# The first norm of a two-layer mixer: shifts as matrix-vector products on TensorE, dot products on VectorE, part of the squares summed on TensorE

## Chip, cores and metric

The program runs on one core of a Trainium2 chip. The metric is the device time of one execution in microseconds (us). A core has a matrix engine (TensorE, PE in the rows, with its weight loads as PEld), a vector engine (VectorE, DVE), a scalar engine (ScalarE, ACT) and a general one (GpSimd, POOL); SyncE (SP) issues the loads. Each takes its instructions in the order in which they were put into its queue and waits for semaphores at the head of the queue.

## What is computed

The reference holds two transformer blocks in sequence; the second follows the first in the same program and is not touched. The change concerns the first norm of the first block's first layer (`S` = 512 tokens, `D` = 1024 channels, all in float32):

```python
def rmsnorm(x, g):
    y = x * lax.rsqrt(jnp.mean(x * x, axis=-1, keepdims=True) + EPS)
    return y * g

c_act = jax.nn.silu(c)
for l in range(DEPTH):
    mod = (c_act @ ada_w[l] + ada_b[l])[:, None, :]
    sh1, sc1, g1, sh2, sc2, g2 = jnp.split(mod, N_MOD, axis=-1)
    h = rmsnorm(x, norm1_g[l]) * (1.0 + sc1) + sh1
    x = x + g1 * token_mix(h, w_in[l], ...)
    ...
```

`token_mix` begins with `h @ w_in`, from which the queries, keys, values and gates of a retention are taken. So the stage needs 1024 shifts (`sh1`) and 1024 scales (`sc1`), each a dot product of 1024 elements with `c_act`, a root of a mean for each token, the normed `h`, and then the first projections.

## The kernel before

**Tiles.** The activations lie transposed: `x[k]`, k = 0 to 7, holds 128 channels on the partitions and 512 tokens along the row. `h[k]` is a pair of such tiles, a high part `hh` (float32 rounded to the matrix engine's fp32r type) and a low part `hl` (what the rounding left). Weights are split the same way: ScalarE makes the high part by a copy (`whi` at L123 for a tile of 128x1024; `yrh` at L140 for halves of 128x512 that are held over the stage), VectorE the low part by a subtraction (`wlo` L124, `yrl` L141). A product in `mm` is three products of 128x128 by 128x512: L151 (hi by hi), L152 (hi by the low part of h), L154 (the low part of the weight by hi).

**The stage `start0` (L923).** It is the head of the program. SyncE loads `x`, a row of `c` for all partitions (`crow`, silu applied), blocks of `ada_w` and the weights.

- Squares: ScalarE squares the eight `x[k]` (L930, L933), VectorE adds them up in seven additions (L934). `rstd_bcast` then sums the result over the partitions by four products with one moving column, one for every 128 tokens (L185), takes the root in seven small operations on VectorE (L164 to L175), and broadcasts it by four products of 128x128 (L193). The broadcast, `R`, stays in the accumulator memory.
- Scales and shifts: a block of `ada_w` comes transposed, 128 channels on the partitions and the 1024 elements of `c` along the row. `mod1` makes one dot product on VectorE (L265: multiply by `crow` and accumulate, 128x1024). Scales (block 8+k) all go this way, and shifts (block k) for k = 0 and 1. For k of 2 and above GpSimd multiplies the shift's block by `crow` (L964) and ScalarE sums the row (L966). Bias additions of 128x1 (L974) and the factor `gm` (L975) follow on VectorE.
- h: `t = x[k]*gm*R` on VectorE (L978), `hh = t + shift` on ScalarE (L979), `hl` on VectorE (L980).
- Products: with each h[k], `mm` for six output tiles: two of queries (weights by `first_w`, one low part on VectorE, one on GpSimd), two of keys and two of gates (weights by `held_w`, split in halves). That is 6 outputs x 8 k x 3 = 144 products of 128x512.

Behind the stage the value projections follow on TensorE; their first product is at L618.

**What sets the order.** The functions only record the work; a scheduler puts the recorded instructions into the queue of each engine, and pools of buffers bound how early a load may go: six slots hold blocks of `ada_w` (pool `stp`), four the raw weights (`raw`). In the queues, an instruction that waits holds up all that stand behind it.

The line that makes a shift for k of 2 and above before:

```python
                pool_e.tensor_tensor(ada[k], ada[k], crow, op=ALU.mult)
                junk = T(D, dt=BF16)
                act.activation(junk, ada[k], AF.Copy, accum_out=raw[:, k:k + 1])
```

Of the kernel before, what the change touches and what calls it, by code (L numbers as in the profile page):

```python
# [11 lines left out]
F32 = mybir.dt.float32  # L12
# [7 lines left out]
P = 128  # L20
# [36 lines left out]
def tile_two_blocks(ctx: ExitStack, tc: tile.TileContext, I, out):  # L57
# [16 lines left out]
    def nm(s):  # L74
        uid[0] += 1
        return f"{s}_{uid[0]}"
# [447 lines left out]

    crow = silu_row(I["c"], crp)
    def x_tile(dt=F32):
        return xp.tile([P, KD * S], dt, tag="x", name=nm("xb"))
# [8 lines left out]
    stp = sts.enter_context(tc.tile_pool(name="stp", bufs=6, side="right"))  # L536

    def ada_load(i):
        t = stp.tile([P, D], F32, tag="ada", name=nm("ada"))
        sp.dma_start(t, I["adaT"][0][i])  # L540
        return t

    ada = {i: ada_load(i) for i in (8, 0)}
# [379 lines left out]
    def start0(mp):  # L923
# [3 lines left out]
        acc = T(S, "t")  # L927
        for k in range(KD):
            if k == 0:
                act.activation(acc, x[k], AF.Square)  # L930
            else:
                sq = T()
                act.activation(sq, x[k], AF.Square)  # L933
                dve.scalar_tensor_tensor(acc, acc, EPS * D / P if k == 1 else 0.0, sq, op0=ALU.add, op1=ALU.add)  # L934
        R = rstd_bcast([(acc, 0)], S)
# [4 lines left out]
        def first_w(m):  # L940
            w = wload(win[m], D, eng=pool_e if m % 2 else dve)
            wks.append([wk(w, k) for k in range(KD)])
# [13 lines left out]
        ada[9], ada[1] = ada_load(9), ada_load(1)  # L956
        held_w(16)
        held_w(17)
        for k in range(KD):
            mod1(0, [8 + k], [ada[8 + k]])  # L960
            if k < 2:
                mod1(0, [k], [ada[k]])
            else:
                pool_e.tensor_tensor(ada[k], ada[k], crow, op=ALU.mult)  # L964
                junk = T(D, dt=BF16)
                act.activation(junk, ada[k], AF.Copy, accum_out=raw[:, k:k + 1])  # L966
            if 2 <= k + 2 < KD:
                ada[10 + k], ada[2 + k] = ada_load(10 + k), ada_load(2 + k)
# [3 lines left out]
            o = COFF["adab"]  # L972
            for i in (8 + k, k):
                dve.tensor_tensor(mod[:, i:i + 1], raw[:, i:i + 1], cols[:, o + i:o + i + 1], op=ALU.add)  # L974
            dve.scalar_tensor_tensor(gm[:, k:k + 1], mod[:, 8 + k:9 + k], 1.0, col("n1g", k),  # L975
# [601 lines left out]
def host_layout(i):  # L1577
# [4 lines left out]
    d["c"] = i["c"].reshape(1, D)  # L1582
    d["c2"] = i["c_2"].reshape(1, D)
# [57 lines left out]
```

## Time and profile before

| | |
|---|---|
| median of three runs | 2994.58 us (2992.69 to 2999.7) |
| profiled execution, its own time | 2997.35 us |
| its span, first to last instruction | 2995.5 us |
| granted clock of TensorE, mean of the span | 0.988 of full |
| TensorE busy | 2913.6 us, 97% |
| VectorE busy | 2128.8 us, 71% |
| ScalarE busy | 1160.0 us, 39% |
| GpSimd busy | 188.3 us, 6% |
| stage `start0` on TensorE | to 73.03 us, start of the first value product |

All rows are of one profiled execution, and their times are microseconds from the start of the span. Busy time counts the instructions that compute. PEclk is the clock that TensorE was granted, as a share of full speed. A float32 product of TensorE that is not of the fp32r type is recorded twice, and with two weight loads, so the four products of L185 stand in the timeline as x8. Operands of TensorE stand as moving data first, then what is loaded as weights; the shape at the end is the output's. Numbers of buffers are left out, and each `ada` is another block. The times of matrix products overlap with their successor's, so the time from start to start is what one of them takes from the next.

### The profile page before, as it was taken

To read this page: it belongs to the slowest core of one execution; us is meant where nothing else is said; L and a number is where in the kernel's file an instruction comes from. 1 tells how busy PE (TensorE), PEld (TensorE's weight loads), DVE (VectorE), ACT (ScalarE), POOL (GpSimd) and SP (SyncE) were. 2 spreads that over 40 slices of the span, in tenths; PEclk is the share of its full clock that TensorE was granted. 3 is DMA by queue.
4 is the path that set the end of the run, shared out by engine and by line. 5 is a ranking of instruction groups with operands and counts; after the bars stand their busy time and mean duration, and the time that the engine had idled before them with its cause. 6 is when DMAs were issued, how large, how long until landed. Compare 5 with 4: busy or idle time off the path is not lost.

```text
span 2995.5 us, 42050 instructions
## 1 busy us (share of the span) xinstructions
PE 2913.6 (97%) x16432; PEld 2562.8 (86%) x16432; DVE 2128.8 (71%) x3765; ACT 1160.0 (39%) x1997; POOL 188.3 (6%) x137
## 2 busy tenths in 40 slices
PE   6999999999999999999999999999999899899998
PEld 4888888988889888888888888999999777899997
DVE  7766455777767665556788878677777767686786
ACT  4333333433344332324433345323334446444442
POOL 2000001000000000002000010000001280200001
PEclk9999999999999999999999999999999899999999
DMA  6444254265553333344355532122224210313331
GB/s 249 126 128 130 96 155 145 89 195 187 187 161 101 116 98 121 120 140 142 114 176 182 168 115 76 64 64 71 71 70 149 70 63 15 99 43 105 107 112 59
DMA packets 119160, 350.41 MB, mean 117 GB/s; under 512 B 12496, under 2 KB 26448, under 8 KB 118960
## 3 DMA queue, kind: packets, MB, share of 16 engines
q1 hardware_dynamic: 117808, 346.67, 36.2%
q8 instruction: 129, 2.11, 0.3%
q10 hardware_dynamic: 1152, 1.05, 0.1%
q14 instruction: 71, 0.58, 0.1%
HBM read 343.48 MB, written 4.19 MB: 116 GB/s over the span
## 4 chain that ended last, share of the span: by engine, by line
PE 91%; DVE 6%; ACT 1%; issue 1%; DMA 1%; POOL 0%; DVEq 0%; SPq 0%; ACTq 0%; POOLq 0%
PE mm L151 28%; PE mm L154 27%; PE mm L152 27%; PE sm L185 1%; PE mm L1438 1%; PE mm L618 1%; PE mm L620 1%; PE mm L619 1%; PE sm L193 1%; DVE acc L219 1%; PE mm L1419 1%; DVE wlo L124 0%; DVE hl L236 0%; PE mm L1241 0%; PE mm L1242 0%
## 5 line engine op out<-in xcount | busy, mean ns | idle before, releaser
L123 ACT ACTIVATE whi<-raw 128x1024 fp32r<-128x1024 f32 (+3 forms) x471 | 453.9, 965 | 775.2 <-PE mm L152 520.3
L151 PE MATMUL mm<-hh,whi 128*128 128x512 f32 (+2 forms) x1956 | 723.7, 371 | 6.5 <-ACT hh L979 4.7
L154 PE MATMUL mm<-hh,wlo 128*128 128x512 f32 (+2 forms) x1956 | 722.9, 370 | 1.4 <-POOL wlo L124 1.4
L152 PE MATMUL mm<-hl,whi 128*128 128x512 f32 (+2 forms) x1956 | 721.7, 369 | 2.2 <-DVE hl L236 2.2
L124 DVE TENSOR_TENSOR wlo<-raw,whi 128x1024 fp32r<-128x1024 f32 (+3 forms) x450 | 497.6, 1111 | 260.8 <-ACT whi L123 256.3
L151 PEld LDWEIGHTS mm<-hh,whi 128*128 128x128 f32 x1956 | 369.6, 189 | 69.6 <-ACT hh L979 5.2
L152 PEld LDWEIGHTS mm<-hl,whi 128*128 128x128 f32 x1956 | 370.2, 189 | 62.3 <-DVE hl L236 3.0
L154 PEld LDWEIGHTS mm<-hh,wlo 128*128 128x128 f32 x1956 | 369.6, 189 | 60.5 <-POOL wlo L124 2.1
L151 PE MATMUL mm<-dh,whi 128*128 128x512 f32 (+1 forms) x760 | 274.8, 362 | 0.0
L152 PE MATMUL mm<-dh,whi 128*128 128x512 f32 (+1 forms) x760 | 268.5, 361 | 0.0
L154 PE MATMUL mm<-dh,wlo 128*128 128x512 f32 (+1 forms) x760 | 251.6, 362 | 0.0
L265 DVE SCALAR_TENSOR_TENSOR t<-ada,crow 128x1024 bf16<-128x1024 f32 x202 | 244.7, 1216 | 6.5 <-DMA ada<-adaT 5.9
L124 POOL TENSOR_TENSOR wlo<-raw,whi 128x1024 fp32r<-128x1024 f32 x21 | 51.7, 2484 | 2309.7 <-ACT whi L123 1764.9
L151 PEld LDWEIGHTS mm<-dh,whi 128*128 128x128 f32 x760 | 143.0, 188 | 29.4
L152 PEld LDWEIGHTS mm<-dh,whi 128*128 128x128 f32 x760 | 142.9, 188 | 23.3
L154 PEld LDWEIGHTS mm<-dh,wlo 128*128 128x128 f32 x760 | 133.1, 188 | 16.7
L847 DVE SCALAR_TENSOR_TENSOR t<-mm,cols,t 128x511 f32<-128x511 f32 (+1 forms) x96 | 70.6, 735 | 73.4 <-ACT t L846 73.0
L151 PE MATMUL mm<-tc,whi 128*128 128x256 f32 (+1 forms) x386 | 113.5, 294 | 0.0
L154 PE MATMUL mm<-tc,wlo 128*128 128x256 f32 (+1 forms) x386 | 112.5, 292 | 0.0
L152 PE MATMUL mm<-tc,whi 128*128 128x256 f32 (+1 forms) x368 | 106.6, 290 | 0.0
L1111 DVE TENSOR_TENSOR z<-z,mm 128x512 f32<-128x512 f32 (+1 forms) x112 | 67.2, 607 | 51.4 <-PE mm L154 51.0
L846 ACT ACTIVATE t<-mm,cols 128x512 f32<-128x512 f32 (+1 forms) x96 | 73.0, 760 | 74.4 <-PE mm L154 74.4
(477 smaller groups left out, 5877.8 us busy)
## 6 DMA issues: line engine op xcount, KB each, us to landing
ada<-adaT SPq DMA_DIRECT2D x96, 512.0 KB, 3.8
raw<-winT SPq DMA_DIRECT2D x96, 512.0 KB, 3.6
raw<-upT SPq DMA_DIRECT2D x88, 512.0 KB, 3.7
raw<-up2T SPq DMA_DIRECT2D x88, 512.0 KB, 3.5
ada<-wmodT SPq DMA_DIRECT2D x72, 512.0 KB, 4.4
raw<-down2T SPq DMA_DIRECT2D x30, 512.0 KB, 4.0
raw<-downT SPq DMA_DIRECT2D x32, 384.0 KB, 3.3
raw<-downT SPq DMA_DIRECT2D x32, 320.0 KB, 3.3
```

The costliest lines, as they stand in the source:

```text
L123: act.activation(hi[:p, :n], raw, AF.Copy)
L124: (eng or dve).tensor_tensor(lo[:p, :n], raw, f(hi[:p, :n]), op=ALU.subtract)
L151: pe.matmul(ps, lhsT=wh, rhs=r[k][0], start=first and k == 0, stop=False, skip_group_check=more)
L152: pe.matmul(ps, lhsT=wh, rhs=r[k][1], start=False, stop=False, skip_group_check=more)
L154: pe.matmul(ps, lhsT=wl, rhs=r[k][0], start=False, stop=last and k == n - 1, skip_group_check=more)
L185: pe.matmul(pm[:, t:t + 1], lhsT=sq[:, t * P:(t + 1) * P], rhs=meanc[:, mc:mc + 1], start=False, stop=i == len(parts) - 1 and t == nt - 1)
L193: pe.matmul(pr[:, t * P:(t + 1) * P], lhsT=y[:, t:t + 1].to_broadcast([P, P]), rhs=identL, start=True, stop=True)
L219: dve.tensor_tensor(acc, acc, sq, op=ALU.add)
L265: dve.scalar_tensor_tensor(junk, raw[:, :D], 1.0, vec, op0=ALU.mult, op1=ALU.mult, accum_out=dst[:, i:i + 1])
L846: act.activation(t, ps, AF.Identity, bias=col(bname, bi), scale=col(wname, taps[1] + wi))
L847: dve.scalar_tensor_tensor(t[:, 1:n], ps[:, 0:n - 1], col(wname, taps[0] + wi), t[:, 1:n], op0=ALU.mult, op1=ALU.add)
L1111: dve.tensor_tensor(zz, zz, ps, op=ALU.add)
```

## The change

Shifts: for all eight k, the block of `ada_w` is loaded in its own orientation (`adaN`, elements of `c` on the partitions) beside the transposed block for the scale, and the shift is eight matrix-vector products on TensorE, each with a 128x128 block as the loaded side and one column of `silu(c)` (`ccol`) as the moving side, all into one column of the accumulator `psh` (L964 in the kernel after). ScalarE adds the bias on its way out (L966). `ccol` is a new small load with its own sigmoid and multiplication.

Scales: the eight dot products on VectorE stay; the bias, plus one, is added once for all (`adab1`), so that `gm` reads the raw dot product. GpSimd does nothing in the stage: its multiplications for the shifts, ScalarE's sums and GpSimd's low part of the second weight go, the last to VectorE.

Squares: `sumsq` with `tail=3` has VectorE add the first five tiles (four additions) and leaves the last three to TensorE, which sums four tiles over the partitions in 16 products instead of one tile in four.

Buffers: the blocks come in pairs, two pairs ahead, from eight slots instead of six.

```diff
--- before.py
+++ after.py
@@ -522,7 +522,12 @@
         pend()
 
 
+    ccol = cst.tile([P, KD], F32, name="ccol")
+    csg = T(8, "se", bufs=4)
+    sp.dma_start(ccol, I["cT"])
     crow = silu_row(I["c"], crp)
+    act.activation(csg, ccol, AF.Sigmoid)
+    dve.tensor_tensor(ccol, ccol, csg, op=ALU.mult)
     def x_tile(dt=F32):
         return xp.tile([P, KD * S], dt, tag="x", name=nm("xb"))
 
@@ -533,14 +538,16 @@
     for k in range(KD):
         sp.dma_start(x[k], I["xT"][:, k * S:(k + 1) * S])
     sts = ExitStack()
-    stp = sts.enter_context(tc.tile_pool(name="stp", bufs=6, side="right"))
-
-    def ada_load(i):
-        t = stp.tile([P, D], F32, tag="ada", name=nm("ada"))
-        sp.dma_start(t, I["adaT"][0][i])
-        return t
-
-    ada = {i: ada_load(i) for i in (8, 0)}
+    stp = sts.enter_context(tc.tile_pool(name="stp", bufs=8, side="right"))
+
+    def ada_load(k):
+
+        ts = [stp.tile([P, D], F32, tag="ada", name=nm("ada")) for _ in (0, 1)]
+        sp.dma_start(ts[0], I["adaT"][0][8 + k])
+        sp.dma_start(ts[1], I["adaN"][k])
+        return ts
+
+    ada = [ada_load(0)]
     cols = cst.tile([P, NCOLS], F32, name="cols")
     sp.dma_start(cols, I["cols"])
     mods = []
@@ -924,21 +931,16 @@
 
 
         raw, mod, gm = mods[0]
-        acc = T(S, "t")
-        for k in range(KD):
-            if k == 0:
-                act.activation(acc, x[k], AF.Square)
-            else:
-                sq = T()
-                act.activation(sq, x[k], AF.Square)
-                dve.scalar_tensor_tensor(acc, acc, EPS * D / P if k == 1 else 0.0, sq, op0=ALU.add, op1=ALU.add)
-        R = rstd_bcast([(acc, 0)], S)
+        R = rstd_bcast(sumsq(x, S, tail=3), S)
+        psh = PS(KD, "sm")
+        adab1 = T(8, "sq1", bufs=4)
+        dve.tensor_scalar(adab1, cols[:, COFF["adab"] + 8:COFF["adab"] + 16], 1.0, None, op0=ALU.add)
         h = hq["h"] = hslots(S)
         win = I["winT"][0]
         wks, pss = [], []
 
         def first_w(m):
-            w = wload(win[m], D, eng=pool_e if m % 2 else dve)
+            w = wload(win[m], D)
             wks.append([wk(w, k) for k in range(KD)])
 
         def held_w(m):
@@ -953,26 +955,21 @@
 
         first_w(8)
         first_w(9)
-        ada[9], ada[1] = ada_load(9), ada_load(1)
+        ada.append(ada_load(1))
         held_w(16)
         held_w(17)
         for k in range(KD):
-            mod1(0, [8 + k], [ada[8 + k]])
-            if k < 2:
-                mod1(0, [k], [ada[k]])
-            else:
-                pool_e.tensor_tensor(ada[k], ada[k], crow, op=ALU.mult)
-                junk = T(D, dt=BF16)
-                act.activation(junk, ada[k], AF.Copy, accum_out=raw[:, k:k + 1])
-            if 2 <= k + 2 < KD:
-                ada[10 + k], ada[2 + k] = ada_load(10 + k), ada_load(2 + k)
+            mod1(0, [8 + k], [ada[k][0]])
+            for i in range(KD):
+                pe.matmul(psh[:, k:k + 1], lhsT=ada[k][1][:, i * P:(i + 1) * P], rhs=ccol[:, i:i + 1],
+                          start=i == 0, stop=i == KD - 1)
+            act.activation(mod[:, k:k + 1], psh[:, k:k + 1], AF.Identity, bias=col("adab", k))
+            if k + 2 < KD:
+                ada.append(ada_load(k + 2))
             if k == 1:
                 held_w(24)
                 held_w(25)
-            o = COFF["adab"]
-            for i in (8 + k, k):
-                dve.tensor_tensor(mod[:, i:i + 1], raw[:, i:i + 1], cols[:, o + i:o + i + 1], op=ALU.add)
-            dve.scalar_tensor_tensor(gm[:, k:k + 1], mod[:, 8 + k:9 + k], 1.0, col("n1g", k),
+            dve.scalar_tensor_tensor(gm[:, k:k + 1], raw[:, 8 + k:9 + k], adab1[:, k:k + 1], col("n1g", k),
                                      op0=ALU.add, op1=ALU.mult)
             tt = T()
             dve.scalar_tensor_tensor(tt, x[k], gm[:, k:k + 1], R, op0=ALU.mult, op1=ALU.mult)
@@ -1580,6 +1577,8 @@
     d["xT"] = i["x"][0].T.reshape(KD, P, S).transpose(1, 0, 2).reshape(P, KD * S)
     d["ctxT"] = i["ctx_2"][0].T.reshape(KD, P, CTX).transpose(1, 0, 2).reshape(P, KD * CTX)
     d["c"] = i["c"].reshape(1, D)
+    d["cT"] = i["c"].reshape(KD, P).T
+    d["adaN"] = i["ada_w"][0][:, 0:D].reshape(KD, P, KD, P).transpose(2, 1, 0, 3).reshape(KD, P, D)
     d["c2"] = i["c_2"].reshape(1, D)
     d["cc"] = i["c_ctx_2"].reshape(1, D)
     pack = {
```

The scheduler places the new instructions as follows. On TensorE, at the head of the program before (`zero`, `meanc` and `identL` are constants, `sm_154` the summed squares, `sm_171` the broadcast, `mm_243` and `mm_247` the two query outputs):

```order
L182 MATMUL sm_154<-zero 128x4
L185 MATMUL sm_154<-meanc,t_131 128x1 x4
L193 MATMUL sm_171<-identL,sy_160 128x128 x4
L182 LDWEIGHTS zero
L182 MATMUL sm_1053<-zero 128x4
L151 MATMUL mm_243<-hh_176,whi_194 128x512
L151 MATMUL mm_247<-hh_176,whi_200 128x512
L152 MATMUL mm_243<-hl_177,whi_194 128x512
```

and after (`acc_136` is the sum of five squares, `t_150` to `t_154` the last three; `ada_117` and `ada_222` are the blocks of the first and second shift):

```order
L185 MATMUL sm_156<-meanc,acc_136 128x1 x4
L185 MATMUL sm_156<-meanc,t_150 128x1 x4
L185 MATMUL sm_156<-meanc,t_152 128x1 x4
L185 MATMUL sm_156<-meanc,t_154 128x1 x4
L193 MATMUL sm_185<-identL,sy_174 128x128 x4
L964 MATMUL sm_190<-ccol,ada_117 128x1 x8
L151 MATMUL mm_265<-hh_193,whi_211 128x512
L152 MATMUL mm_265<-hl_194,whi_211 128x512
L154 MATMUL mm_265<-hh_193,wlo_212 128x512
L151 MATMUL mm_269<-hh_193,whi_217 128x512
L152 MATMUL mm_269<-hl_194,whi_217 128x512
L154 MATMUL mm_269<-hh_193,wlo_218 128x512
L964 MATMUL sm_190<-ccol,ada_222 128x1 x8
```

Three groups of four products have come ahead of the broadcast, and eight matrix-vector products stand ahead of the first product with h; the next eight stand behind the last product of k = 0.

On ScalarE, from the last square on, before:

```order
L933 ACTIVATE t_151<-xb_99 128x512
L123 ACTIVATE whi_194<-raw_192 128x1024
L979 ACTIVATE hh_176<-t_239,mod_118 128x512
L123 ACTIVATE whi_200<-raw_198 128x1024
L140 ACTIVATE yrh_210<-raw_208 128x512
L140 ACTIVATE yrh_214<-raw_208 128x512
L979 ACTIVATE hh_178<-t_290,mod_118 128x512
```

and after:

```order
L210 ACTIVATE t_154<-xb_104 128x512
L966 ACTIVATE mod_123<-sm_190,cols 128x1
L976 ACTIVATE hh_193<-t_261,mod_123 128x512
L123 ACTIVATE whi_211<-raw_209 128x1024
L123 ACTIVATE whi_217<-raw_215 128x1024
L966 ACTIVATE mod_123<-sm_190,cols 128x1
L976 ACTIVATE hh_195<-t_317,mod_123 128x512
```

The high part of the first weight (`whi`) stood ahead of the first h tile and now stands behind it and behind the shift's bias (L966).

On VectorE the first dot product stood ahead of the root and the second within it; now one dot product stands within the root, ahead of its last step, and none ahead of it.

On TensorE in the middle of the stage, from the last product of k = 3 to the first ones of k = 4, before:

```order
L152 MATMUL mm_307<-hl_183,yrh_279 128x512
L154 MATMUL mm_307<-hh_182,yrl_280 128x512
L151 MATMUL mm_243<-hh_184,whi_194 128x512
L152 MATMUL mm_243<-hl_185,whi_194 128x512
L154 MATMUL mm_243<-hh_184,wlo_195 128x512
```

and after (k = 4 is `hh_201`; `ada_347` and `ada_397` are the blocks of the shifts of k = 4 and 5):

```order
L154 MATMUL mm_334<-hh_199,yrl_309 128x512
L964 MATMUL sm_190<-ccol,ada_347 128x1 x8
L964 MATMUL sm_190<-ccol,ada_397 128x1 x8
L151 MATMUL mm_265<-hh_201,whi_211 128x512
L151 MATMUL mm_269<-hh_201,whi_217 128x512
```

Two groups of eight matrix-vector products stand back to back between the products of k = 3 and those of k = 4.

## Rows read from the trace of the kernel before

**Rows 1.** page part 1: busy us of each engine, share of span, instructions.

```profile
PE 2913.6 (97%) x16432; PEld 2562.8 (86%) x16432; DVE 2128.8 (71%) x3765; ACT 1160.0 (39%) x1997; POOL 188.3 (6%) x137
```

**Rows 2.** stretches: from:to, length, busy us (instructions) of PE, PEld, DVE, ACT, POOL, PEclk, DMA, GB/s.

```profile
20.00:30.00 10.00, 4.51 (x8) 2.29 (x8) 9.93 (x10) 2.60 (x4) 8.36 (x3) 1.00 1.03 402
40.00:50.00 10.00, 6.84 (x26) 5.26 (x27) 9.67 (x9) 4.99 (x10) 5.14 (x2) 0.94 0.43 156
```

**Rows 3.** TensorE's waits, 0 to 140 us: total us, times, longest us.

```profile
PE sm L185 <- DVE t L934: 11.6, 1, 11.6
PE mm L154 <- DVE yrl L141: 7.5, 2, 4.6
PE mm L151 <- ACT hh L979: 4.7, 2, 3.2
```

**Rows 4.** timeline of TensorE: start, us, line, operation, operands, xcount, [idle before <-releaser].

```profile
48.79 0.74 PE L154 MATMUL mm<-hh,yrl 128*128 128x512 f32 x1 [2.90 <-DVE yrl L141]
...
73.03 0.28 PE L618 MATMUL mm<-whi,hh 128*128 128x256 f32 x1
```

**Rows 5.** chain of waits, 45 to 60 us: start, us until the next, what.

```profile
49.53 0.43 PE mm L151
...
53.17 0.23 PE mm L152
...
59.93 0.23 PE mm L151
```

**Rows 6.** timelines of GpSimd (first row) and VectorE.

```profile
21.64 3.36 POOL L124 TENSOR_TENSOR wlo<-raw,whi 128x1024 fp32r<-128x1024 f32 x1 [20.34 <-ACT whi L123]
...
22.84 2.18 DVE L974 TENSOR_TENSOR mod<-modr,cols 128x1 f32<-128x1 f32 x1
...
30.60 1.28 DVE L141 TENSOR_TENSOR yrl<-raw,yrh 128x512 fp32r<-128x512 f32 x2
...
32.47 3.46 DVE L141 TENSOR_TENSOR yrl<-raw,yrh 128x512 fp32r<-128x512 f32 x2
```

**Rows 7.** timeline of VectorE, 8 to 20 us.

```profile
8.14 4.67 DVE L934 SCALAR_TENSOR_TENSOR t<-t,t 128x512 f32<-128x512 f32 x6
...
12.73 1.22 DVE L265 SCALAR_TENSOR_TENSOR t<-ada,crow 128x1024 bf16<-128x1024 f32 x1
...
14.77 0.16 DVE L164 TENSOR_SCALAR sy<-sm 128x4 int32<-128x4 int32 x1 [0.81 <-PE sm L185]
...
19.11 0.75 DVE L978 SCALAR_TENSOR_TENSOR t<-xb,gm,sm 128x512 f32<-128x512 f32 x1 [2.17 <-PE sm L193]
```

**Rows 8.** timeline of TensorE, 12 to 21 us and 123 to 125 us.

```profile
12.87 1.86 PE L185 MATMUL sm<-meanc,t 128*128 128x1 f32 x8 [11.62 <-DVE t L934]
17.00 2.08 PE L193 MATMUL sm<-identL,sy 128*128 128x128 f32 x8 [2.27 <-DVE sy L175]
...
20.67 0.79 PE L151 MATMUL mm<-hh,whi 128*128 128x512 f32 x1 [1.48 <-ACT hh L979]
...
123.19 0.95 PE L185 MATMUL sm<-meanc,acc 128*128 128x1 f32 x8
124.01 0.37 PE L618 MATMUL mm<-whi,hh 128*128 128x256 f32 x1
```

**Rows 9.** timeline of ScalarE, 15 to 32 us.

```profile
15.41 1.06 ACT L123 ACTIVATE whi<-raw 128x1024 fp32r<-128x1024 f32 x1 [3.99 <-DMA raw<-winT]
19.89 0.72 ACT L979 ACTIVATE hh<-t,mod 128x512 fp32r<-128x512 f32 x1 [3.43 <-DVE t L978]
...
30.71 0.72 ACT L979 ACTIVATE hh<-t,mod 128x512 fp32r<-128x512 f32 x1 [8.11 <-DVE mod L974]
```

**Rows 10.** a stage far behind: TensorE's timeline, then two adjoining stretches.

```profile
1168.63 0.39 PE L748 MATMUL mm<-dftg,ue 128*128 128x65 f32 x2
...
1168.45:1171.86 3.41, 3.16 (x29) 3.03 (x28) 2.08 (x5) 0.75 (x3) 0.00 (x0) 1.00 0.49 151
1171.86:1175.27 3.41, 3.41 (x17) 3.41 (x18) 1.50 (x5) 1.21 (x4) 0.00 (x0) 0.50 0.22 89
```

## The prediction

> **What bounds the kernel now.** I read the page's busy shares first: TensorE is busy for 97% of the span [rows 1], so the end moves only by idle or slow time of TensorE. The table by stretches shows that the touched stage is where it still idles: 4.51 us busy of the 10 us from 20 to 30, 6.84 of those from 40 to 50, while VectorE is busy 9.93 and 9.67 in the first two [rows 2]. TensorE's list of waits up to 140 us names who it waits for: the summed squares (11.6 us), two low parts of weights (7.5 us) and two h tiles (4.7 us) [rows 3]. Its last wait ends at 48.79; the timeline has no gap behind it up to the first value product (L618) at 73.03 [rows 4]. Behind that row the orders of both kernels agree instruction by instruction on TensorE (and, within some twenty microseconds of it, on VectorE and ScalarE). So the reader is to look for one number: **when TensorE reaches that first value product, now 73.03 us.** Whatever it is later or earlier goes into the end.
>
> The stage has 144 products of 128x512. [...] By counting in the order, 47 are done at 48.79 and 97 remain: seven at 0.43 and ninety at 0.233 make 24.0, and 48.79 + 24.0 = 72.8, as seen.
>
> **What the change takes away.** GpSimd's share goes. It stood in VectorE's way: while GpSimd held its low part from 21.64 for 3.36 us, a 128x1 addition on VectorE took 2.18 us and ended with it; two low halves took 3.46 us beside GpSimd's work and 1.28 us without it [rows 6]. Summed over the seven stretched instructions of the stage some 14 us of VectorE go. So do three of the seven adds of squares (4.67 us for six, 0.78 each) and two of the ten dot products (1.22 us each) [rows 7]; a low part of 1.2 to 1.3 us, as the two halves now take [rows 6], comes to VectorE. The loads are the same in bytes (a shift's 512 KB block for another), and two more slots let them be issued earlier. All of this feeds TensorE sooner, if nothing else is late.
>
> **What it adds.** TensorE gets 64 products with one moving column for the shifts and 12 more for the squares. The trace has that form: four in 1.86 us at the start of the kernel, 0.46 each, and four in 0.82 us (123.19 to 124.01) amid dense work, 0.205 each [rows 8]. So 64 cost 13.1 us at the high clock and 29.8 us at the low one. [...]
>
> Now the walk, in the order that each queue has in the changed kernel.
> 1. Squares. VectorE's four adds end about 10.9 us: three fewer than before's end at 12.8 [rows 7, 8], with 0.4 us for the small column load and sigmoid ahead. Then 16 products instead of four: 16 x 0.46 = 7.4, so 18.3, against 14.7 now. These were a single wait of TensorE; moving adds there makes the sum later, since the engine is at its low clock.
> 2. The root and its broadcast. VectorE took 2.2 us, from 14.77 to the broadcast's start at 17.00, one dot product of 1.22 in it [rows 7, 8]; the new order has one dot product inside the chain too, though VectorE idles for 7 us before it. The broadcast is 2.08 us [rows 8]. x times R starts at about 22.6, now 19.11.
> 3. The first shift. Eight products at 0.46 are 3.7 us, to 26.3; ScalarE adds the bias (0.2 us, an estimate from the 0.16 us of a 128x4 operation on VectorE [rows 7]) and makes the first h tile, 0.72 us, to 27.2, where it was made at 19.89. The high part of the first weight was made at 15.41, ahead of it; now it is queued behind the wait for the shift on ScalarE [rows 9], and the first big product starts at 28.2 instead of 20.67 [rows 8]. **The stage starts 7.5 us late.**
> 4. Step k=1. VectorE makes two low parts (1.2 to 1.3 each), a dot product and x times R: about 33. The eight products of k=1 stand behind the last product of k=0, which waits for the second low part (30.7): to 34.9; second h tile at 35.2, now 30.71 [rows 9].
> 5. Steps k=2 and 3. Without GpSimd four low halves take 2.6 us. Eighteen products, two more groups of shifts (1.6 to 3.7 us each): TensorE is dense from about 48, between 46 and 50 by the clock. 28 products of 128x512 are done, 116 remain (97 at the same time before).
> 6. From there TensorE is its own bound: 116 x 0.233 = 27.1, the shifts of k=4 to 7, 32 x 0.205 = 6.6, and one stall of about 1 us, because the group for k=7 is queued behind the products of k=6, and its h tile is made only after it. 48.2 + 34.7 = 82.9.
> 7. The clock. The dense stretch holds groups of up to 16 one-column products in a row. Between 1168.45 and 1171.86 TensorE was busy for 3.16 us of 3.41 with products of 63 to 65 columns (weights of 128 each), and the granted clock was 0.50 for the next 3.41 us [rows 10]. So products that stream little do not hold the clock. A fall costs 7 x 0.2 = 1.4 us in the stretch at 48.79 [rows 5] and up to 1.7 us; short products within it cost 0.26 more each. Two to three falls: 4.5 us (bounds 0 and 11).
>
> Sum: 87.4 us instead of 73.0, **14.4 us more**. On the profiled execution's 2997.35 us (span 2995.5 and 1.85 around it) that is 3011.8; it lies 2.8 us above the median of the runs, 2994.58, so the forecast is 3009 us. Downstream I cost nothing: the loads have more time, and TensorE is dense to 120. If the clock takes its least and most, the walk ends between 81.5 and 92: 3003 to 3014.
>
> **Rivals.** *Not slower.* The one-column products keep the clock up: 0.205 each almost from the start. Then step 1 ends 2.3 us sooner, steps 3 and 4 two each, step 5 four: dense at 37.7, and 34.7 more with 1.5 for the cold start make 73.9, at most 77: 2995 to 2998 us. It decides if the granted clock stays 1.00 through the first shifts. Against it speak rows 10; for it only that TensorE has few idle gaps here. [...]
>
> *Slower still.* The short groups find the low clock each time in the second half also: 32 x 0.26 = 8.3 us on top, 95.7, some 3017 us. For it: groups k=4 and 5 stand back to back.
>
> *Faster.* VectorE's relief decides alone: TensorE is dense from the 20.67 us of now: 144 x 0.233 and 56 x 0.205 are 45.1, so 65.8, 7.3 us sooner, 2987 us. It needs the root no later and the high clock throughout; steps 1 and 3 speak against it, and it is the floor of all that can be gained.
>
> **How the numbers follow.** Forecast 0.67, not slower 0.17, slower still 0.13, faster 0.03. The bound between a difference and none is 0.2%, 6 us, about what a measurement here can tell. Above 3000.6 lie nearly all of the forecast (0.64) and the slower rival: 0.77; within, 0.20; faster 0.03. The range goes from 2997, into the first rival, to 3017, into the second.
>
> **What would show it.** Right: four groups of squares' products ending near 18; first big product near 28; groups L964 of 3 to 4 us at the start; granted clock at 0.50 in some stretches between 40 and 85; first value product (L625) near 87; no stretched VectorE instruction. Step 7 is wrong if that product stands near 75 with the clock at 1.00; steps 3 to 5 if TensorE is dense before 40. The forecast is wrong in kind if, behind that product, TensorE's waits differ from now.

## The result and the profile after

The kernel after takes 3017.74 us (median of four runs, 3016.8 to 3020.0) against 2995.86 us of before on the same chip: ratio 1.0068, 95% interval 1.0056 to 1.008. It is slower by 21.9 us. The forecast of 14.4 us more had the sign, the place and the mechanism, and was a third too small: 3017.74 lies 0.7 us above the top of the stated range, which was counted from a median of before 1.3 us below the one here.

The profiled execution took 3017.32 us, its span 3015.5, 20.0 more than before. The busy shares, which answer to [rows 1]:

```profile
PE 2944.8 (98%) x16584; PEld 2594.6 (86%) x16584; DVE 2108.8 (70%) x3745; ACT 1155.3 (38%) x1994; POOL 168.7 (6%) x130
```

TensorE is busy for 31 us more: 19.8 for the products of the shifts (eight groups, of which the one at 39.82 is left out below), 5.3 for twelve more of the squares, the rest, some 6 us, for the same products, which take 0.43 us each instead of 0.23 in the falls of the clock below. GpSimd and VectorE have 20 us less each.

TensorE's timeline through the stage (start, us until its modelled end, line, operation, [idle before <-releaser]; x16 is eight products of a shift, x8 are four of the squares or the broadcast):

```profile
11.10 1.87 PE L185 MATMUL sm<-meanc,acc 128*128 128x1 f32 x8 [9.86 <-DVE acc L219]
12.83 5.26 PE L185 MATMUL sm<-meanc,t 128*128 128x1 f32 x24
20.35 2.08 PE L193 MATMUL sm<-identL,sy 128*128 128x128 f32 x8 [2.26 <-DVE sy L175]
22.22 3.41 PE L964 MATMUL sm<-ccol,ada 128*128 128x1 f32 x16
27.68 0.79 PE L151 MATMUL mm<-hh,whi 128*128 128x512 f32 x1 [2.05 <-ACT whi L123]
...
30.81 2.01 PE L964 MATMUL sm<-ccol,ada 128*128 128x1 f32 x16
33.92 0.74 PE L151 MATMUL mm<-hh,whi 128*128 128x512 f32 x2 [1.10 <-ACT hh L976]
...
43.80 2.48 PE L964 MATMUL sm<-ccol,ada 128*128 128x1 f32 x16
...
58.95 1.84 PE L964 MATMUL sm<-ccol,ada 128*128 128x1 f32 x16
61.15 2.94 PE L964 MATMUL sm<-ccol,ada 128*128 128x1 f32 x16 [0.35 <-ACT mod L966]
63.95 1.20 PE L151 MATMUL mm<-hh,whi 128*128 128x512 f32 x2
...
66.65 3.41 PE L964 MATMUL sm<-ccol,ada 128*128 128x1 f32 x16
69.92 0.77 PE L152 MATMUL mm<-hl,whi 128*128 128x512 f32 x1
...
83.70 1.84 PE L964 MATMUL sm<-ccol,ada 128*128 128x1 f32 x16
...
86.65 0.73 PE L151 MATMUL mm<-hh,whi 128*128 128x512 f32 x2 [1.00 <-ACT hh L976]
...
91.68 0.39 PE L625 MATMUL mm<-whi,hh 128*128 128x256 f32 x1 [0.58 <-DVE t L599]
```

The number to look for is the last: the first value product starts at 91.68, where it stood at 73.03 [rows 4]. That is 18.65 of the 20.0 us between the two spans; the other 1.35 us lie behind it. There TensorE has the same products in the same order in both kernels, 16,270 records each, and the distance of a product from its counterpart wanders between 15.4 and 23.2 us before it ends at 20.0. At two places of it the clock differs: from 1172.0 to 1175.5 us the kernel before was granted 0.53, and the same products of the kernel after, at 1190.6 to 1194.1, 1.00; from 1424.0 to 1428.4 it was 1.00 in the kernel before, and 0.71 at 1442.0 to 1447.5 in the kernel after. So a microsecond or two between two single executions says nothing of the stage.

The groups at 22.22, 43.80, 61.15 and 66.65 are longer than the 1.84 us of the same eight products at 58.95: the clock is down there. For the last three the table by stretches (columns as in [rows 2]) shows it; for the first the record reads 1.00, and only the time of the products tells (see the last section):

```profile
20.00:30.00 10.00, 7.56 (x29) 6.53 (x29) 4.43 (x10) 2.87 (x4) 0.00 (x0) 1.00 0.75 285
...
40.00:50.00 10.00, 8.89 (x44) 7.86 (x45) 4.65 (x10) 4.04 (x8) 0.00 (x0) 0.74 0.68 243
50.00:60.00 10.00, 10.00 (x47) 8.21 (x46) 5.88 (x11) 0.00 (x0) 0.00 (x0) 0.92 0.44 173
60.00:70.00 10.00, 9.65 (x47) 8.98 (x46) 3.52 (x6) 1.97 (x4) 0.00 (x0) 0.59 0.01 2
70.00:80.00 10.00, 10.00 (x34) 7.96 (x34) 3.90 (x5) 2.88 (x4) 0.00 (x0) 0.72 0.33 105
```

TensorE is the busier engine now in every one of these rows, and VectorE, which was at 9.93 and 9.67 of ten [rows 2], is now busy for 3.5 to 5.9 of ten. The bound of the stage has moved from VectorE to TensorE, which is granted 0.59 to 0.92 of its full clock in each ten microseconds from 40 to 80. Products of 128x512 stand 0.43 us apart in three falls: from 34.5 to 37.9 us, from 46.7 to 51.4, and from 64 to 75.2 with the group at 66.65 in it. VectorE's relief is real; its low halves are no longer stretched (four in 2.49 us, where two took 3.46 [rows 6]):

```profile
34.57 2.49 DVE L141 TENSOR_TENSOR yrl<-raw,yrh 128x512 fp32r<-128x512 f32 x4
```

### The profile page after: what moved, and what is told of

The parts are those of the page before. It is cut to its first block, busy times and chain, and to the rows that moved or that the text cites. A ratio compares the mean times of both kernels' runs of the same rounds, so it can differ in the third digit from the quotient of the medians.

```text
span 3015.5 us, 42316 instructions
## 1 busy us (share of the span) xinstructions
PE 2944.8 (98%) x16584; PEld 2594.6 (86%) x16584; DVE 2108.8 (70%) x3745; ACT 1155.3 (38%) x1994; POOL 168.7 (6%) x130
## 4 chain that ended last, share of the span: by engine, by line
PE 93%; DVE 4%; ACT 1%; DMA 1%; issue 0%; POOL 0%; SPq 0%; DVEq 0%; ACTq 0%; POOLq 0%
PE mm L151 28%; PE mm L152 27%; PE mm L154 27%; PE sm L185 1%; PE mm L1435 1%; PE mm L625 1%; PE mm L627 1%; PE mm L626 1%; PE sm L193 1%; PE sm L964 1%; PE mm L1416 1%; DVE acc L219 0%; PE mm L1238 0%; PE mm L1239 0%; DVE wlo L124 0%
## 5 line engine op out<-in xcount | busy, mean ns | idle before, releaser
L152 PEld LDWEIGHTS mm<-dh,whi 128*128 128x128 f32 x760 | 143.5, 189 | 23.2
```

The source lines that it names most:

```text
L152: pe.matmul(ps, lhsT=wh, rhs=r[k][1], start=False, stop=False, skip_group_check=more)
```

## The experiments

The theory: the one-column products cost TensorE their own time and, placed in groups, bring its clock down, so that the products of 128x512 behind them are slow too. The rivals: the loss is the later start (the squares on TensorE, the first shift ahead of the first h tile); GpSimd's help is what is missing; the clock falls because of the waits, not the products. All ratios are to the kernel before on the same chip (its medians: 2995.86 for the kernel after, 2997.86, 2998.45 and 2998.16 for the rest), with 95% intervals. "First value product" is the start of the row that stands at 73.03 us before and at 91.68 after.

| kernel | first value product, us | median, us | ratio to before |
|---|---|---|---|
| before | 73.03 | 2995.86 | |
| after | 91.68 | 3017.74 | 1.0068 (1.0056 to 1.008) |
| sq_vec | 90.88 | 3016.31 | 1.0066 (1.0054 to 1.0078) |
| wide_first | 93.37 | 3015.87 | 1.0052 (1.0035 to 1.0069) |
| wide64 | 86.31 | 3011.34 | 1.004 (1.0027 to 1.0053) |
| spread | 84.78 | 3008.96 | 1.0033 (1.0023 to 1.0044) |
| wide128 | 81.99 | 3009.11 | 1.0043 (1.003 to 1.0056) |
| half | 78.04 | 3007.13 | 1.0027 (1.0017 to 1.0038) |
| dot_vec | 66.04 | 2991.78 | 0.9981 (0.9972 to 0.9989) |
| dot_sq_6 | 62.95 | 2987.94 | 0.9962 (0.995 to 0.9975) |
| dot_sq_vec | 62.92 | 2990.14 | 0.9976 (0.9967 to 0.9985) |

Against before on the same chip, each time differs by as much as the stage does, to within 4 us, over a range of 30 us. Whatever is gained or lost there goes into the end, as the prediction had it.

### The squares back on VectorE (sq_vec)

```diff
-        R = rstd_bcast(sumsq(x, S, tail=3), S)
+        R = rstd_bcast(sumsq(x, S, tail=0), S)
```

> The kernel after with one part undone: all seven additions of squares back on VectorE, four products for the sum instead of 16. If the squares on TensorE lie on the path, their sum ends near 14.8 us instead of 18.1, all of the stage moves up by about 3.3 us, the first value product (L625) comes near 88.4 us instead of 91.7 and the time is about 3014.5 us. If something else is late there (the first blocks or weights landing), the stage starts where it does now and the time stays at 3017 to 3018 us.

It gave neither. TensorE's timeline in this kernel:

```profile
13.80 1.87 PE L185 MATMUL sm<-meanc,acc 128*128 128x1 f32 x8 [12.56 <-DVE acc L219]
...
25.11 0.80 PE L151 MATMUL mm<-hh,whi 128*128 128x512 f32 x1 [1.91 <-ACT hh L976]
...
28.36 3.41 PE L964 MATMUL sm<-ccol,ada 128*128 128x1 f32 x16
...
90.88 0.38 PE L625 MATMUL mm<-whi,hh 128*128 128x256 f32 x1 [0.61 <-DVE t L599]
```

The sum ends at 15.67 instead of 18.09 and the first big product starts 2.6 us sooner. Then it is given back: the shift of k = 1 takes 3.41 us instead of 2.01, because in the kernel after the clock rises within that group, while here the products stay 0.43 us apart until 36.9 us. At the first value product 0.8 us are left, and the time does not differ from that of after. So the 2.6 us that the squares cost at the start were on the path there and worth little at the end of the stage, while TensorE is the bound.

### Shifts as dot products on VectorE (dot_vec, dot_sq_vec, dot_sq_6)

```diff
-        sp.dma_start(ts[1], I["adaN"][k])
+        sp.dma_start(ts[1], I["adaT"][0][k])
...
-            for i in range(KD):
-                pe.matmul(psh[:, k:k + 1], lhsT=ada[k][1][:, i * P:(i + 1) * P], rhs=ccol[:, i:i + 1],
-                          start=i == 0, stop=i == KD - 1)
-            act.activation(mod[:, k:k + 1], psh[:, k:k + 1], AF.Identity, bias=col("adab", k))
+            mod1(0, [k], [ada[k][1]])
+            act.activation(mod[:, k:k + 1], raw[:, k:k + 1], AF.Identity, bias=col("adab", k))
```

> The kernel after with the other part undone: no matrix-vector products, all eight shifts as dot products on VectorE (1.22 us each), GpSimd still idle, squares still on TensorE. If the one-column products, in their own time (19.8 us in all) and in the low clock behind them, are the loss, VectorE becomes the bound of the stage: some 38 us of work from 22.5 us on, to about 61, the first value product comes near 67 us (65 to 70) and the time is 2991 to 2996 us. If the loss were in the later start or in GpSimd's missing help, VectorE with eight more dot products is later still, the first value product stays behind 80 us and the time above 3005 us.

```profile
66.04 0.28 PE L625 MATMUL mm<-whi,hh 128*128 128x256 f32 x1
```

The first value product came at 66.04 us and the time at 2991.78: without the matrix-vector products the stage is 25.6 us shorter, with eight more dot products on VectorE and GpSimd still idle. The granted clock is 1.00 in every ten microseconds from 10 to 80, although up to 35.7 us the products still stand 0.43 apart, as at the head of the other kernels. This settles the largest question: the products on TensorE are the loss, neither GpSimd's missing help nor the squares, which are on TensorE here too. The first shift is gone from the start with the others; that is worth 2.8 us there (first big product at 24.88 instead of 27.68).

With the squares on VectorE too (the edit of sq_vec on top):

> Both undone, so that against the kernel before GpSimd's work alone is moved to VectorE (and two more slots for blocks). If GpSimd's stretching of VectorE was the larger harm, the stage is shorter than before: first value product at 62 to 67 us against 73.0, time 2988 to 2991 us, faster than before by 0.2%. If its help was worth more than the stretching, the first value product comes behind 75 us and the time is above 2998 us.

62.92 us, 2990.14, faster than before. Here the squares' 3.1 us (66.04 less 62.92) come through to the end of the stage; the intervals of the two times overlap. Against the kernel before, this run differs in GpSimd's work (and ScalarE's sums behind it), now on VectorE, in the additions of the biases, and in two more slots. What it does for VectorE is seen in the groups of the two kernels up to the end of the stage (line, operation, xcount | busy us, mean ns of one | idle before). First before, then this run:

```profile
L141 DVE TENSOR_TENSOR yrl<-raw,yrh 128x512 fp32r<-128x512 f32 x8 | 11.7, 1498 | 0.1
L980 DVE SCALAR_TENSOR_TENSOR hl<-t,mod,hh 128x512 fp32r<-128x512 f32 x8 | 7.7, 964 | 1.4 <-ACT hh L979 1.4
...
L974 DVE TENSOR_TENSOR mod<-modr,cols 128x1 f32<-128x1 f32 x16 | 5.8, 372 | 0.1
...
L975 DVE SCALAR_TENSOR_TENSOR gm<-mod,cols 128x1 f32<-128x1 f32 x8 | 3.4, 423 | 0.2
```

```profile
L265 DVE SCALAR_TENSOR_TENSOR t<-ada,crow 128x1024 bf16<-128x1024 f32 x16 | 19.3, 1219 | 0.0
L974 DVE SCALAR_TENSOR_TENSOR hl<-t,mod,hh 128x512 fp32r<-128x512 f32 x8 | 6.0, 747 | 0.0
...
L141 DVE TENSOR_TENSOR yrl<-raw,yrh 128x512 fp32r<-128x512 f32 x8 | 5.2, 685 | 0.0
...
L969 DVE SCALAR_TENSOR_TENSOR gm<-modr,sq,cols 128x1 f32<-128x1 f32 x8 | 1.7, 217 | 0.0
```

The same eight low halves take 5.2 us instead of 11.7, the low parts of h 6.0 instead of 7.7, and the small operations 1.7 instead of 9.2: 15.7 us less, for six dot products (7.3 us) and one low part (1.2 us) more. Of the 15.7, the edit itself saves about 1.8 by dropping 16 additions (two that nothing stretched took 0.22 us at 16.06); some 14 are GpSimd's doing. The traces show it in the single operations: a low half took 1498 ns in the mean in the kernel before and 685 with GpSimd idle, and the addition of [rows 6] ended at 25.02, when GpSimd's operation ended at 25.00.

Whether it was the two slots:

```diff
-    stp = sts.enter_context(tc.tile_pool(name="stp", bufs=8, side="right"))
+    stp = sts.enter_context(tc.tile_pool(name="stp", bufs=6, side="right"))
```

> The run with dot products and squares on VectorE, with six slots for blocks as in the kernel before instead of eight; the order on VectorE is the same. If the gain over the kernel before comes from VectorE working without GpSimd, the first value product stays within a microsecond of 62.9 us and the time at 2988 to 2992 us. If it comes from the earlier loads, blocks land late, VectorE waits for them, and the first value product comes at 66 us or later, time at 2993 us or more.

62.95 us, 2987.94: the slots do nothing that can be measured, since the two intervals overlap. Both versions are faster than before, by 0.2 to 0.4%, and so faster than after by about 1%.

### Half of the one-column products (half)

```diff
-            for i in range(KD):
+            for i in range(0, KD, 2):
...
-                          start=i == 0, stop=i == KD - 1)
+                          start=i == 0, stop=i == KD - 2)
```

> The kernel after with every second block of each shift left out (four one-column products in each group instead of eight), everything else and the order of all engines unchanged. The eight groups take 19.8 us now. If they only cost their own time at the high clock, half of them is 32 x 0.205 = 6.6 us: first value product near 85 us, time near 3011 us. If they also bring the clock down and the shorter groups do not, up to 10 us more of products at the low clock come back: first value product at 76 to 80 us, time 3001 to 3006 us.

```profile
78.04 0.38 PE L625 MATMUL mm<-whi,hh 128*128 128x256 f32 x1 [0.58 <-DVE t L599]
```

The kernel leaves out half of every shift and is for timing only. The first value product came at 78.04 us, 13.6 sooner, more than twice the 6.6 us that 32 products cost at the high clock. The groups themselves take 9.6 us instead of 19.8, so 10.2 of the 13.6 are theirs, at either clock, and the rest is what stands behind them. Against before on the same chip the kernel is 8.7 us slower, where after is 21.9; in absolute time, 3007.13, it lies a microsecond above what the theory gave. In this run the second half of the stage has one short fall of the clock, behind the groups of k = 4 and 5 (0.50 from 57 to 59 us, 1.00 again from 61 on), instead of the long one from 61 to 75.

### More columns (wide128, wide64)

```diff
+            r = (k % 4) * 128
...
-                pe.matmul(psh[:, k:k + 1], lhsT=ada[k][1][:, i * P:(i + 1) * P], rhs=ccol[:, i:i + 1],
-                          start=i == 0, stop=i == KD - 1)
+                pe.matmul(psh[:, r:r + 128], lhsT=ada[k][1][:, i * P:(i + 1) * P],
+                          rhs=ccol[:, i:i + 1].to_broadcast([P, 128]), start=i == 0, stop=i == KD - 1)
```

> The kernel after with one size changed: each matrix-vector product streams 128 copies of its column instead of one, with the same loads. If the clock falls because the products stream little, the granted clock stays at 1.00 from 38 us on, the groups of eight take 2.0 to 2.2 us each instead of up to 3.4, the loss of some 10 us behind 44 us goes and 3 us of streaming come: first value product near 85 us, time near 3011 us. If the clock does not hang on that, the 64 products only become dearer: first value product near 95 us, time near 3021 us.

```profile
40.00:50.00 10.00, 9.41 (x47) 7.71 (x48) 7.98 (x14) 3.36 (x8) 0.00 (x0) 1.00 0.70 244
...
60.00:70.00 10.00, 9.40 (x54) 7.87 (x53) 1.24 (x2) 1.65 (x4) 0.00 (x0) 1.00 0.33 105
```

With 128 times the streaming the kernel is 11.2 us slower than before on the same chip, where after is 21.9 (the two intervals meet only at their ends): the clock is 1.00 from 40 us on, and the first value product at 81.99, better than forecast, since the wider products cost next to nothing (the first group of eight takes 3.42 us, with one column 3.41; at the high clock 1.95 and 1.84). But the scheduler, which takes the wide products for longer ones, also cut the groups from k = 3 on, those of k = 4 and later in two halves with 18 products between. (The second half of one shift then stands right ahead of the first half of the next, with a wait of 0.35 us between them.) The columns alone did not keep the clock up either: behind the first group of 128 columns, which stood uncut, and waits of 1.10 and 0.45 us the products came 0.23 us apart from 28.50 to 28.96, but 0.47 and 0.59 from there, the second group took 3.18 us, and the granted clock was 0.96 in the mean from 20 to 30 us and 0.87 from 30 to 40. So this run alone does not say whether the columns or the cutting held the clock. With 64 columns:

> As the run with 128 columns, with 64. Its groups are cut much as there (two and six instead of four and four). If what is streamed sets the clock, 64 columns, which did not hold it in the rows of before with 63 to 65 columns, give an outcome between: stretches below 1.00 remain behind the groups of eight up to 45 us and perhaps one or two of those of six, time 3008 to 3013 us. If only the cutting of the groups mattered, the clock behind 45 us is 1.00 as with 128 columns, and the time is at or a little below the 3009 us measured there.

The clock was 1.00 from 40 us on here too, so that the groups of this run, cut much in the same way, held as well; its first value product is later than with 128 columns because the clock rose first at 40 us (products 0.43 us apart up to 40.20, 0.24 from there). By the clock that is the expectation's second case, by the time, 3011.34, its first; it told the two apart no better. (The intervals of these two runs overlap.)

### One column, cut groups (spread)

```diff
+                    n = 3 if k < 2 else 2
+                    shift(k + 1, todo[:n])
+                    todo = todo[n:]
```

(`shift` makes the products of the listed blocks; the lines stand behind each call of `mm`.)

> The kernel after with its one-column products placed otherwise: from the shift of k = 4 on, two at a time among the products of the step before instead of eight or sixteen in a row (the shifts of k = 0 to 3 stay in groups of eight). Nothing is added or taken away. If the clock falls because TensorE streams little over a group, the granted clock stays at 1.00 from about 52 us on, each product costs 0.2 us, the stall at 60 to 61 us goes, and the 8 to 9 us lost between 60 and 87 us come back: first value product near 83 us, time near 3009 us. If one-column products bring the clock down wherever they stand, stretches at 0.50 remain behind 52 us and the time stays above 3014 us.

```profile
45.56 3.27 PE L958 MATMUL sm<-ccol,ada 128*128 128x1 f32 x16
...
57.48 0.50 PE L958 MATMUL sm<-ccol,ada 128*128 128x1 f32 x4
...
84.78 0.28 PE L625 MATMUL mm<-whi,hh 128*128 128x256 f32 x1
```

The group at 45.56, still in one piece, is slow as in the kernel after; the pairs from 57.48 on are fast (0.37 us to the next start), the clock is 1.00 from 60 us to 100, and the first value product comes 6.9 us sooner. One-column products do not bring the clock down wherever they stand: it is the group, and not each time. The scheduler left the eight products of k = 7 in one piece here too (74.45, no wait behind them), and the clock stayed at 1.00.

### More columns, groups uncut (wide_first), and a probe

```diff
+            n = 64 if k in (0, 1, 2) else 1
```

> The kernel after with the products of the first three shifts streaming 64 copies of their column; the order of every engine is that of the kernel after, and the groups are not cut. If what is streamed sets the clock, the fall at 44 us, which followed the group of k = 2, does not come: products behind it 0.23 us apart, first value product 3 to 5 us sooner (87 to 89 us), time 3013 to 3015 us; the falls behind k = 4 to 6, still one column, remain. If only long groups and gaps matter, the fall at 44 us stays and the time is 3017 to 3019 us.

```profile
46.27 2.15 PE L969 MATMUL sm<-ccol,ada 128*128 128x1 f32 x16
...
84.60 1.84 PE L969 MATMUL sm<-ccol,ada 128*128 128x1 f32 x16
```

A miss. The fall came after all, but later: not at 44 us behind the group of k = 2 (64 columns), but behind that of k = 3 (one column), whose eight products took 2.15 us from 46.27 on before those of 128x512 went 0.43 apart. The groups of k = 0 and 1 ran at the low clock with 64 columns also (3.52 and 3.51 us, where the one of k = 2 took 1.89), and the products came 0.43 us apart until 40.4 us. The profiled execution's stage was 1.7 us longer than after's, and its median 1.9 us below; the intervals overlap. (Of the 1.7 us, 0.8 lie behind the group of k = 7, at 84.60: from the end of the wait behind it, at 87.55, it is 5.82 us to the first value product, in the kernel after 5.03, from 86.65.) Since one group with one column was left right behind, it does not decide.

So the products were measured by themselves, in a program that has only them, with nothing else on TensorE and no scheduler's choice: 56 products of 128x512 between groups.

```python
    def group(n, cols):
        ...
        for i in range(n):
            b = i % KD
            pe.matmul(psh[:, 0:cols], lhsT=ada[:, b * P:(b + 1) * P], rhs=rhs, start=True, stop=True)
    ...
    for cols in (1, 64, 128):
        for n in (8, 16, 32):
            group(n, cols)
            dense(56)
    for cols in (1, 64, 128):
        for n in (8, 16):
            group(n, cols)
            gap(psh[:, 0:1])
            dense(56)
```

> A probe that leaves out the whole computation (its output is a copy of the input) and runs on TensorE alone: stretches of 56 products of 128x512, and between them groups of 8, 16 and 32 products of the shift's form with 1, 64 and 128 columns moving; then groups of 8 and 16 followed by a wait of about a microsecond for two instructions on ScalarE, as in the stage; then two one-column products and three of 128x512 in turn, 16 times. If what is streamed sets the clock, the one-column groups of 16 and 32 are followed by granted clock 0.50 and 0.43 us from product to product, the groups of 128 columns are not, 64 stands between, and two in turn with three hold 1.00. If only gaps count, no group without a wait is followed by 0.50 and all groups with a wait are, whatever their columns.

TensorE's timeline of the probe (L92 is the group, L84 are the 56 products behind it, whose second number is 13.08 at full clock):

```profile
40.60 1.84 PE L92 MATMUL psh<-hh,ada 128*128 128x1 f32 x16
42.30 13.08 PE L84 MATMUL mm<-hh,whi 128*128 128x512 f32 x56
55.22 4.01 PE L92 MATMUL psh<-hh,ada 128*128 128x1 f32 x32
59.09 15.89 PE L84 MATMUL mm<-hh,whi 128*128 128x512 f32 x56
...
114.25 3.68 PE L92 MATMUL psh<-hh,ada 128*128 128x64 f32 x32
117.74 13.08 PE L84 MATMUL mm<-hh,whi 128*128 128x512 f32 x56
...
181.65 7.30 PE L92 MATMUL psh<-hh,ada 128*128 128x128 f32 x64
188.71 13.31 PE L84 MATMUL mm<-hh,whi 128*128 128x512 f32 x56
201.86 1.84 PE L92 MATMUL psh<-hh,ada 128*128 128x1 f32 x16
204.72 14.68 PE L84 MATMUL mm<-hh,whi 128*128 128x512 f32 x56 [1.01 <-ACT hh L76]
...
239.46 1.89 PE L92 MATMUL psh<-hh,ada 128*128 128x64 f32 x16
242.37 14.67 PE L84 MATMUL mm<-hh,whi 128*128 128x512 f32 x56 [1.01 <-ACT hh L76]
...
274.50 1.95 PE L92 MATMUL psh<-hh,ada 128*128 128x128 f32 x16
277.46 13.11 PE L84 MATMUL mm<-hh,whi 128*128 128x512 f32 x56 [1.01 <-ACT hh L76]
```

And two stretches of its table (columns: stretch, length, busy PE, PEld, ACT, POOL, PEclk, DMA, GB/s): behind the 16 one-column products, and all of the part in which pairs alternate with three products.

```profile
59.10:63.10 4.00, 4.00 (x11) 3.13 (x12) 0.00 (x0) 0.00 (x0) 0.50 0.00 0
...
322.00:341.00 19.00, 19.00 (x116) 16.71 (x115) 0.00 (x0) 0.00 (x0) 1.00 0.00 0
```

In the probe both matter, the streaming and the wait. Eight one-column products without a wait left the clock up. Sixteen, with no idle time on either side, brought it down: 0.50 behind them, 2.8 us lost in the next 56 products and 0.5 in the group; so did thirty-two (15.09 us behind them). Groups of 16 and 32 with 64 or 128 columns did not (13.31 us behind the longest, with the clock at 1.00 there). A wait of 1.01 us with only products of 128x512 around it did not either; the same wait behind eight one-column products did (1.6 us), behind eight of 64 columns also, behind eight of 128 not. Pairs among the big products held 1.00 throughout. In the kernel before a wait alone did cost the clock: behind the one of 2.90 us that ended at 48.79 [rows 4], with only products of 128x512 around it, they stood 0.43 us apart (behind the one of 3.18 us that ended at 40.27 they did not: 0.23 from 41.30 on). In the probe the wait of 1.01 us cost it only behind small products, and the fall at 55 us has no gap at all.

This is one execution on one chip; the counts are what was seen, not limits. The stage itself shows that they are no rule. In the kernel after, the eight one-column products of k = 7 with a wait of 1.00 us behind them (83.70 and 86.65) were followed by 1.00 up to 100 us, and so were they in sq_vec; in wide_first the same products behind the same group and wait (84.60) took 0.8 us longer up to the first value product (5.82 us instead of 5.03). In wide64 eight products of 64 columns in one piece (42.07) with a wait of 1.11 us behind were followed by 1.00, in the probe such a group was not. What else decides is not shown here.

## Why the prediction was right, point by point

- **What bounds it.** Right: the difference is the start of the first value product, 18.65 us later, of 20.0 between the two spans. The change in the later stages was put at nothing; it was 1.35 us in the profiled executions, which had different clocks for the same products at two places (0.53 against 1.00, 1.00 against 0.71). TensorE's waits behind that product are those of before, as forecast.
- **Steps 1 to 3, the later start.** Right to half a microsecond: sum at 18.09 (18.3 forecast), first big product at 27.68 (28.2). The price of 0.46 us at the low clock, read from four products in [rows 8], held nearly for all 16 of the squares (from 11.10 to 18.09, 0.44 each) and for the first shift (3.41, forecast 3.7). What the step did not see is that the start's worth is not kept: sq_vec took 2.6 us of it back and had 0.8 at the end of the stage.
- **Steps 4 and 5.** Too late by about 2 us: the clock rose within the second group, which took 2.01 instead of 3.7 us. The state forecast for 48.2 us (four shifts and 28 products of 128x512 done) was reached at 46.14, and 33 were done at 48.42. The last wait ahead of the dense stretch ended at 42.77 already, outside the 46 to 50 that were stated.
- **Step 6.** Right in kind: from 48.42 on, without any fall of the clock, 111 products at 0.233 are 25.9 us, 32 one-column products at 0.205 are 6.6, and three waits (0.35, 1.00 and 0.58 us; 1.0 forecast) 1.9, together 34.4, to 82.8. (The 0.233 is the mean of the 29 products from 53.17 to 59.93 of [rows 5], whose 0.43 is the distance behind the wait at 48.79.)
- **Step 7, the clock: the term that was mis-sized.** The first value product came at 91.68, so the clock cost 8.9 us from there on, and not 4.5; the bound of 11 held it. (The walk's ends as recorded, 81.5 and 92, are not what its bounds give: 82.9 plus 0 and plus 11 are 82.9 and 93.9.) It is made up of the groups of k = 5 and 6 (2.80 us from 61.15 to the next product and 3.27 from 66.65, instead of 1.64 each: 2.8), twelve products from 69.92 to 75.18 (5.26 instead of 2.80: 2.5), six from 63.95 to 66.65 (1.3), eight from 48.42 to 51.75 (1.5) and small ends (0.6, an estimate): 8.7 of the 8.9. The step counted falls as short ones, each with a cost of its own. From 61 to 75 us there was a single long one, and the group of k = 6, at 66.65, ran within it: the price of a fall depends on what follows it.
- **The rivals.** "Not slower" needed 0.205 us for each one-column product almost from the start; the first shift took 0.43 each, so it did not come. The sign that was named for it, a granted clock of 1.00 through the first shifts, was a bad one: the record does read 1.00 from 20 to 30 us. That few idle gaps speak for it rests on one place of the kernel before, the 0.43 us behind the wait at 48.79; the probe's fall at 55 us came without a gap. The rival's 1.5 us for the start are the author's estimate, and no run shows them. (Its sum also slips a little: 48.2 less the 10.3 us named is 37.9, not 37.7.) "Slower still" was half of what happened: of the last four groups those of k = 5 and 6 found the low clock, those of k = 4 and 7 did not (1.84 us each); its time, some 3017, is nearly the one measured, though its 95.7 us for the stage is too much. "Faster" fell for the change as a whole, but its mechanism exists: with GpSimd idle and no one-column products on TensorE for the shifts the stage ended at 62.92 us, sooner than the 65.8 that it had as the floor, in which 56 such products were counted.
- **What the change takes away.** The 14 us of stretched work on VectorE are borne out: some 14 by the groups of dot_sq_vec. That it feeds TensorE sooner did not help, since the one-column products stood ahead.

The rest of the gap, 21.9 us by the medians against 20.0 by the profiled executions, is within what runs of the kernel before differ among themselves (2992.69 to 2999.7).

## What to carry to other kernels

A float32 matrix-vector product on TensorE came with two weight loads here and took 0.21 us (eight in 1.70), and a group of 16 also slowed what stood behind it (56 products in 15.89 us instead of 13.08): put a few at a time among the large products, as in spread, where the clock was 1.00 from 60 us on, or keep the dot products on an engine with room. Where such groups can't be avoided, more columns were nearly free here (1.95 us for eight of 128, 1.84 for eight of one), and the clock held behind all five groups of 128 in the probe (13.07 to 13.31 us) and from 40 us on in wide128, though not behind the first group there. Before a helper engine is used, see what it does to the engine that it is to relieve: here GpSimd took 8.5 us of work from VectorE and cost it some 14.

## What the runs showed of the hardware that was not expected

- A product with two weight loads of 128 columns cost the same with 1, 64 or 128 float32 columns moving: eight took 1.70 us from start to next start in all three cases of the probe (40.60 to 42.30, 99.63 to 101.33, 150.63 to 152.33).
- TensorE's first stretch of work was slow without the record of the granted clock saying so: from 20 to 30 us of the kernel after it reads 1.00, while products stand 0.43 us apart (29.53, 29.96, 30.38). At the head of these programs the distance of the products is the measure.
- A longer group can bring the clock down less than a shorter one: with 64 columns and the wait, the 56 products behind eight took 14.67 us, those behind 16 took 13.09. The runs do not say why.
- The same products in the same order can lose the clock in one execution and keep it in another: 0.53 from 1172.0 to 1175.5 us of the kernel before, 1.00 for the same products of the kernel after (1190.6 to 1194.1).
